# Reordering the first transfers of a hybrid attention/RWKV block: token rows and first weights first, vector rows from ScalarE's queue, unit blocks and bias rows later

## The chip, the cores and the metric

The kernel runs on one core of a Trainium2 chip. The metric is the device time of one execution in microseconds (us). Before the change it is 3353.46 us, the median of three runs (3352.36 to 3354.02). A core has TensorE (matmul, "PE"), VectorE ("DVE"), ScalarE ("ACT"), GpSimd ("POOL") and SyncE ("SP"), which here only issues DMA transfers. ScalarE and GpSimd issue some transfers too. All engines run their own instruction list in order and wait for each other by semaphores.

## The reference

One layer for 2048 tokens of width 1024: a norm, one projection to 5376 columns, chunk-band attention and an RWKV-7 recurrence on its parts, a gated merge, and a feed-forward part.

```python
h = rms_norm(x, pre_mix_g)
proj = h @ w_in                                  # 1024 x 5376
p_att, p_rwkv, p_gate = columns of proj          # 1536, 1792, 2048
y_a = chunk_band_attention(p_att, rel_bias)      # bias by clipped distance
y_b = rwkv7_time_mix(p_rwkv, shift_mu, w0, w2, a0, a2, g2, k_k, k_a, r_k, ln_x_w, ln_x_b)
merged = sigmoid(gate_a) * (y_a @ proj_a) + sigmoid(gate_b) * (y_b @ proj_b)
x = x + rms_norm(merged @ w_out, post_mix_g)
x = x + rms_norm(relu(rms_norm(x, pre_ffn_g) @ w_up)**2 @ w_down, post_ffn_g)
```

## The kernel before

The tokens are worked in four groups of 512 (`G`). For each group the kernel keeps the normed tokens h transposed in SBUF, split into a rounded part and its rest (`hh`, `hl`), and multiplies them with weight blocks of 128 columns. A weight block is 512 KB. SyncE loads it into a buffer `raw` (two of them), ScalarE casts it to `whi` (line 69), VectorE subtracts to `wlo` (line 70), and TensorE adds up 3 x 8 products of 128x128 by 128x512 in one PSUM bank `psd` (line 78): `hh,whi`, `hl,whi` and `hh,wlo` for each of the eight parts of 128 rows. There are two buffers each of `raw`, `whi` and `wlo`, so the load of a block waits until VectorE has read the block two before it, and its cast waits until TensorE is through with that block. Each transfer also uses one of eight completion counters (DMAHW0 to DMAHW7), which are given out in turn over the queues of SyncE and ScalarE; a transfer is not issued before the last one on its counter has landed.

Where a group starts, `phase_norm` loads four tiles of 128 token rows and the gains `g_pre` (each 512 KB), ScalarE sums the squares (line 303), GpSimd makes `rs_r` from them (lines 123 and 125), VectorE scales the tile in place (line 306), TensorE transposes it (line 144), ScalarE casts to `hh` (line 146) and VectorE subtracts to `hl` (line 147). Only the first group does this at the start of the program; for the other groups it lies beside earlier work.

`constants` builds what the mixing needs. It loads nine vectors as rows of one tile `rows` (line 216), which TensorE transposes into `cst` (line 225); the small matrices w2 and a2 (line 223); eight parts of `x0`, a block of unit columns by which the triangular inverse starts (line 242; ScalarE copies it to `X` at line 535); and, in `build_bias`, eight copies of 384 KB that spread each head's bias row 128 times in DRAM (`skew`, line 898), from which the attention phase reads its bias tiles much later.

After that `phase_rwkv` runs for the group. Its first column blocks are the low-rank inputs (`lora_wa`, column block 12, called block 1 below), then r, k and v of head pair 0 (blocks 2 to 4), two gate blocks (5 and 6), and r, k and v of pair 1 (7 to 9); block 10 is the next gate block. From block 1 come `lw` and `lora`, which the small products `ps_z` and `ps_a` (lines 355 and 356) need; from `ps_z` come `tw`, a scan over it (line 396) and `E` (line 400).

A scheduler orders each engine's instructions by its own estimates, within what the data and the buffers allow. So the place of an instruction in its engine's list is not always its place in the code.

Of the kernel before, what the change touches and what calls it, by code (L numbers as in the profile page):

```python
# [8 lines left out]
F32 = mybir.dt.float32  # L9
# [8 lines left out]
P = 128  # L18
D = 1024
# [4 lines left out]
G = 512  # L24
GT = G // P
# [15 lines left out]
RW0 = 1536  # L41
# [3 lines left out]
def advance(steps, n=None):  # L45

    while n is None or n > 0:
        if next(steps, steps) is steps:
            return
        n = n and n - 1  # L50


class Block:
# [5 lines left out]

    def wsplit(self, src, k, n):  # L60

        raw = self.wp.tile([P, k, n], F32, tag="raw", name="wraw")
        self.nc.sync.dma_start(raw, src)
        hi, lo = (self.wp.tile([P, k, n], F32R, tag="w" + x, name="w" + x) for x in ("hi", "lo"))
        self.split(hi, lo, raw)
        return hi, lo
# [41 lines left out]
    def dense(self, col):  # L108


        if self.g == 0:
            self.order.append(col)
            wh, wl = self.wsplit(*self.block(col))
        else:
            wh, wl = next(self.feed)
        ps = self.pd.tile([P, G], F32, tag="d", name="psd")
        self.mm = self.mm3(ps, [(wh[:, k], wl[:, k], self.h[0][:, k], self.h[1][:, k]) for k in range(KB)])
        return ps
# [31 lines left out]
    def constants(self, ctx, mixing):  # L150
        tc, nc, a = self.tc, self.nc, self.a
# [53 lines left out]
        with tc.tile_pool(name="setup", bufs=1, side="right") as sp, \  # L205
# [5 lines left out]
            )  # L211
            yield
            raw = sp.tile([nrow, P], F32, name="rows")
            at, off = 0, {}
            for name, n in rows:
                nc.sync.dma_start(raw[at : at + n], a[name].rearrange("(n p) -> n p", p=P))
                off[name] = at
                at += n
            raw2 = []
            for x in ("w2", "a2"):  # L220
# [7 lines left out]
            for par in range(2):  # L228
# [6 lines left out]
                )  # L235
            self.build_bias(sp, dp)
            eyeb = sp.tile([2, 512], BF16, name="eyeb")
            nc.vector.tensor_copy(eyeb, eye.rearrange("p r j -> p (r j)"))
            eyed = dp.tile([2, 512], BF16, name="eyed")
            nc.sync.dma_start(eyed, eyeb)  # L240
            for i in range(8):
                nc.sync.dma_start(
                    self.x0[i * 16 : i * 16 + 16].rearrange("p r j -> p (r j)"),
                    eyed[i % 2][None, :].to_broadcast((16, 512)),
                )

        def view(name, n):
# [47 lines left out]

    def norm_steps(self, g, sp, pt, gt, t):

        nc = self.nc
        x = sp.tile([P, D], F32, tag="x", bufs=GT, name="x")
        nc.sync.dma_start(x, self.a["x"][g * G + t * P : g * G + (t + 1) * P])  # L300
        sq = sp.tile([P, D], F32, tag="sq", bufs=1, name="sqx")
# [11 lines left out]
    def phase_norm(self, g, sp, pt):  # L313

        gt = self.gain(sp, self.a["pre_mix_g"], "g_pre")
        for t in range(GT):
            advance(self.norm_steps(g, sp, pt, gt, t))

# [53 lines left out]
    def rwkv_pre(self, g, p, rp, NA, between=lambda: None):  # L372
        nc = self.nc
# [17 lines left out]
        self.mix(g, 8 + p, v)  # L391

        between()
        nc.vector.tensor_scalar(tw, tw, -0.5 * DEC, -0.5 * DEC, ALU.mult, ALU.add)
# [490 lines left out]
    def build_bias(self, sp, dp):  # L885
# [10 lines left out]
        nc.sync.dma_start(band, ext)  # L896
        for h in range(8):
            nc.sync.dma_start(
                self.skew[h].rearrange("(q m) -> q m", m=769)[:, 0:768], band[h][None, :].to_broadcast((P, 768))
            )  # L900

# [577 lines left out]
    def run(self):  # L1479
        tc, e = self.tc, None  # L1480
        with ExitStack() as ctx, ExitStack() as mixing:
            e = mixing.enter_context
            consts = self.constants(ctx, mixing)
            advance(consts, 1)
            self.pd = ctx.enter_context(tc.tile_pool(name="pd", bufs=2, space=PSUM))
            self.wp = e(tc.tile_pool(name="w", bufs=2))
# [83 lines left out]
```

## Time and profile before

| | |
|---|---|
| median of three runs | 3353.46 us (3352.36 to 3354.02) |
| the profiled execution's own time | 3355.02 us |
| its span, first to last instruction | 3353.1 us |
| mean granted TensorE clock | 0.991 |
| moved by DMA | 478.42 MB, mean 143 GB/s |
| eight `skew` copies | 384.0 KB each, issued by SyncE |

The page divides the span into 40 slices and gives the busy tenths of each engine in each. A row of a group or of the timeline names line, engine, operation, out<-in and shape; what stands in square brackets is the time that the engine was idle before it, and the instruction or transfer that ended this idle time. In the rows of stretches the columns are: the stretch and its length, busy time and count for PE, PEld, DVE, ACT and POOL, the granted TensorE clock, the busy share of the DMA engines, and GB/s. A row with SPq is the issue of a transfer on SyncE, not the transfer.

### The profile page before, as it was taken

How to read it: one execution, taken by the hardware profiler on the slowest of the kernel's cores; microseconds unless marked ns; L12 is line 12 of the kernel's file. 1: busy time of each engine (PE TensorE's matmuls, PEld its weight loads, DVE VectorE, ACT ScalarE, POOL GpSimd, SP SyncE). 2: the span in 40 equal slices, each digit the busy share in tenths (PEclk: the TensorE clock that was granted, in tenths of full speed). 3: DMA queues.
4: the chain of work that ended last, by engine and by line, in shares of the span. 5: the costliest groups of instructions: out<-in, count | busy, mean ns of one | idle time of the engine just before them, and what ended most of it. 6: DMA issues, size and time to landing. Idle time of an engine off the chain costs nothing. (4 is left out here: it accounts for less than half of the span.)

```text
span 3353.1 us, 49354 instructions
## 1 busy us (share of the span) xinstructions
PE 3254.7 (97%) x19089; PEld 2612.5 (78%) x19089; DVE 2281.7 (68%) x3806; ACT 1461.6 (44%) x2331; POOL 391.8 (12%) x732
## 2 busy tenths in 40 slices
PE   7999999999999999999999999999999999999998
PEld 5777777777777778777777777888887877888886
DVE  5774656675665774665774675876877777776778
ACT  3434634444644434644434644333331254454432
POOL 2110002110012210012210000111200011100002
PEclk9999999999999999999999999999999999999999
DMA  4224343125364224354224266334755364554443
GB/s 150 86 78 149 105 138 117 64 95 175 97 222 133 76 86 165 107 203 151 83 82 152 86 216 228 131 115 141 269 174 200 109 240 162 171 169 154 148 154 126
DMA packets 164945, 478.42 MB, mean 143 GB/s; under 512 B 17436, under 2 KB 34016, under 8 KB 162024
## 3 DMA queue, kind: packets, MB, share of 16 engines
q1 hardware_dynamic: 110120, 364.10, 33.3%
q0 software_dynamic: 18688, 63.98, 4.9%
q10 hardware_dynamic: 35904, 47.20, 3.9%
q8 instruction: 151, 2.47, 0.3%
q14 instruction: 82, 0.67, 0.1%
HBM read 355.64 MB, written 122.71 MB: 143 GB/s over the span
## 5 line engine op out<-in xcount | busy, mean ns | idle before, releaser
L78 PE MATMUL psd<-hh,whi 128*128 128x512 f32 x1344 | 545.2, 406 | 8.9 <-ACT whi L69 6.6
L78 PE MATMUL psd<-hl,whi 128*128 128x512 f32 x1344 | 541.6, 403 | 0.0
L78 PE MATMUL psd<-hh,wlo 128*128 128x512 f32 x1344 | 539.4, 401 | 0.6 <-DVE wlo L70 0.5
L69 ACT CAST whi<-wraw 128x1024 fp32r<-128x1024 f32 x232 | 243.5, 1050 | 530.7 <-PE psd L78 423.2
L78 PE MATMUL ps_dn<-fop 128*128 128x512 f32 x1920 | 440.7, 390 | 3.5 <-DVE u L1267 2.9
L70 DVE TENSOR_TENSOR wlo<-wraw,whi 128x1024 fp32r<-128x1024 f32 x232 | 283.0, 1220 | 213.5 <-ACT whi L69 193.8
L78 PEld LDWEIGHTS ps_dn<-fop 128*128 128x128 f32 x1920 | 359.0, 188 | 81.3 <-DVE u L1267 4.9
L78 PEld LDWEIGHTS psd<-hh,whi 128*128 128x128 f32 x1344 | 257.1, 191 | 65.1 <-ACT whi L69 7.4
L78 PEld LDWEIGHTS psd<-hh,wlo 128*128 128x128 f32 x1344 | 257.0, 191 | 56.6 <-issue 3.5
L78 PEld LDWEIGHTS psd<-hl,whi 128*128 128x128 f32 x1344 | 257.1, 191 | 51.3 <-issue 2.1
L78 PE MATMUL ps_dn<-fop,fop 128*128 128x512 f32 x1008 | 228.6, 389 | 0.0
L78 PEld LDWEIGHTS ps_dn<-fop,fop 128*128 128x128 f32 x1008 | 189.2, 188 | 39.3
L1267 DVE TENSOR_TENSOR u<-u,ps_dn 128x512 f32<-128x512 f32 x240 | 160.0, 682 | 51.9 <-PE ps_dn L78 51.2
L868 DVE CUSTOM_DVE_ANT_0 sc<-bias,ps_s 128x640 f32<-128x640 f32 (+4 forms) x128 | 94.1, 735 | 55.4 <-PE ps_s L862 47.1
L69 ACT CAST fop<-wdraw 128x1024 fp32r<-128x1024 f32 x40 | 41.9, 1047 | 191.4 <-DVE u L1267 106.9
L873 ACT ACTIVATE sc<-sc,mn 128x640 f32<-128x640 f32 (+4 forms) x128 | 97.8, 764 | 35.3 <-DVE mn L868 30.1
L69 ACT CAST s12h<-s 128x1024 fp32r<-128x1024 f32 x32 | 33.7, 1053 | 169.4 <-PE ps_u L78 164.6
L995 PE MATMUL ps_o<-whi,mh 128*128 128x512 f32 x256 | 102.6, 401 | 2.4 <-ACT o L1001 2.4
L995 PE MATMUL ps_o<-wlo,mh 128*128 128x512 f32 x256 | 102.3, 400 | 0.5 <-DVE wlo L70 0.4
L78 PE MATMUL ps_p<-yh,whi 128*128 128x512 f32 x256 | 101.9, 398 | 0.6 <-DVE th L961 0.6
L78 PE MATMUL ps_p<-yh,wlo 128*128 128x512 f32 x256 | 102.2, 399 | 0.0
L995 PE MATMUL ps_o<-whi,ml 128*128 128x512 f32 x256 | 101.7, 397 | 0.0
(378 smaller groups left out, 6751.1 us busy)
## 6 DMA issues: line engine op xcount, KB each, us to landing
wraw<-in_w_in_dram SPq DMA_DIRECT2D x168, 512.0 KB
wraw<-in_w_up_dram SPq DMA_DIRECT2D x80, 512.0 KB
ar<-sd SPq DMA_DIRECT2D x21, 1024.0 KB
wdraw<-in_w_down_dram SPq DMA_DIRECT2D x40, 512.0 KB
araw<-ad SPq DMA_DIRECT2D x40, 512.0 KB
gd<-gate ACTq DMA_DIRECT2D x64, 256.0 KB
wraw<-in_w_out_dram SPq DMA_DIRECT2D x32, 512.0 KB
ad<-r POOLq DMA_DIRECT2D x64, 256.0 KB, 2.7
```

Source lines behind the costliest of these rows:

```text
L69: self.nc.scalar.copy(hi, src)
L70: self.nc.vector.tensor_tensor(lo, src, hi.bitcast(F32), ALU.subtract)
L78: mm = nc.tensor.matmul(ps, l, r, start=start and n == 0, stop=stop and n == last).ins
L868: nc.vector.tensor_tensor_reduce(sc[:, 0:n], bias[:, s0:640], pss[:, c0 : c0 + n], 1.0, 3.0e38, ALU.add, ALU.min, mn,)
L873: nc.scalar.activation(sc[:, 0:n], sc[:, 0:n], AF.Exp, scale=-1.0, bias=mn, accum_out=sm)
L995: nc.tensor.matmul(ps[t], l[:, k, ts], r[:, k % 2], start=k == 0 and j == 0, stop=k == KB - 1 and j == 2)
L1267: nc.vector.tensor_tensor(u[t][:, ns], u[t][:, ns], ps, ALU.add)
```

## The change

The load of a weight block and its split are parted, so that the load can be written earlier than the split. `phase_norm` now issues the four token tiles, then the gains, then the loads of blocks 1 and 2, and splits these blocks after the norm. The nine vector rows are issued by ScalarE instead of SyncE, ahead of all other work of ScalarE. The eight `x0` copies and the eight `skew` copies go into a generator `spread` that `rwkv_pre` runs for head pairs 0 and 1 of the first group: `x0` for pair 0 and `skew` for pair 1, each batch placed behind the weight load that was written last. The products, their count and the order of the weight blocks stay.

```diff
...
         self.NG = self.S // G
 
 
-    def wsplit(self, src, k, n):
-
+    def wload(self, src, k, n):
         raw = self.wp.tile([P, k, n], F32, tag="raw", name="wraw")
-        self.nc.sync.dma_start(raw, src)
+        self.loaded = self.nc.sync.dma_start(raw, src).ins
+        return raw, k, n
+
+    def wsplit(self, *block):
+        return self.wparts(*self.wload(*block))
+
+    def wparts(self, raw, k, n):
         hi, lo = (self.wp.tile([P, k, n], F32R, tag="w" + x, name="w" + x) for x in ("hi", "lo"))
         self.split(hi, lo, raw)
         return hi, lo
...
 
         if self.g == 0:
             self.order.append(col)
-            wh, wl = self.wsplit(*self.block(col))
+            wh, wl = self.first.pop(col, None) or self.wsplit(*self.block(col))
         else:
             wh, wl = next(self.feed)
         ps = self.pd.tile([P, G], F32, tag="d", name="psd")
...
             nc.gpsimd.affine_select(
                 eye, eye, [[1, 32], [-2, 16]], ALU.is_equal, 0.0, base=0, channel_multiplier=-1
             )
-            yield
             raw = sp.tile([nrow, P], F32, name="rows")
             at, off = 0, {}
             for name, n in rows:
-                nc.sync.dma_start(raw[at : at + n], a[name].rearrange("(n p) -> n p", p=P))
+                nc.scalar.dma_start(raw[at : at + n], a[name].rearrange("(n p) -> n p", p=P))
                 off[name] = at
                 at += n
+            yield
             raw2 = []
             for x in ("w2", "a2"):
                 raw2.append(sp.tile([P, HW], F32, name="raw2"+x))
...
                 nc.vector.tensor_tensor(
                     self.wl[par][r], raw2[par][r], self.wh[par][r].bitcast(F32), ALU.subtract
                 )
-            self.build_bias(sp, dp)
+            band = self.build_bias(sp, dp)
             eyeb = sp.tile([2, 512], BF16, name="eyeb")
             nc.vector.tensor_copy(eyeb, eye.rearrange("p r j -> p (r j)"))
             eyed = dp.tile([2, 512], BF16, name="eyed")
             nc.sync.dma_start(eyed, eyeb)
+
+        def spread():
             for i in range(8):
                 nc.sync.dma_start(
                     self.x0[i * 16 : i * 16 + 16].rearrange("p r j -> p (r j)"),
                     eyed[i % 2][None, :].to_broadcast((16, 512)),
                 )
+                yield
+            for h in range(8):
+                nc.sync.dma_start(
+                    self.skew[h].rearrange("(q m) -> q m", m=769)[:, 0:768], band[h][None, :].to_broadcast((P, 768))
+                )
+                yield
+
+        self.spread = spread()
 
         def view(name, n):
             return self.cst[:, off[name] : off[name] + n]
...
         lo = self.hp.tile([P, KB, G], F32R, tag="hl", name="hl")
         return hi, lo
 
-    def norm_steps(self, g, sp, pt, gt, t):
+    def norm_load(self, g, sp, t):
+        x = sp.tile([P, D], F32, tag="x", bufs=GT, name="x")
+        self.nc.sync.dma_start(x, self.a["x"][g * G + t * P : g * G + (t + 1) * P])
+        return x
+
+    def norm_steps(self, g, sp, pt, gt, t, x=None):
 
         nc = self.nc
-        x = sp.tile([P, D], F32, tag="x", bufs=GT, name="x")
-        nc.sync.dma_start(x, self.a["x"][g * G + t * P : g * G + (t + 1) * P])
+        if x is None:
+            x = self.norm_load(g, sp, t)
         sq = sp.tile([P, D], F32, tag="sq", bufs=1, name="sqx")
         ssq = sp.tile([P, 1], F32, tag="ssq", bufs=4, name="ssq")
         nc.scalar.activation(sq, x, AF.Square, accum_out=ssq)
...
 
     def phase_norm(self, g, sp, pt):
 
+        xs = [self.norm_load(g, sp, t) for t in range(GT)]
         gt = self.gain(sp, self.a["pre_mix_g"], "g_pre")
+        first = [(col, self.wload(*self.block(col))) for col in (RW0 + 12 * P, RW0)]
         for t in range(GT):
-            advance(self.norm_steps(g, sp, pt, gt, t))
+            advance(self.norm_steps(g, sp, pt, gt, t, xs[t]))
+        for col, w in first:
+            self.first[col] = self.wparts(*w)
 
 
     def mix(self, g, blk, out):
...
         v = self.tmp("v")
         self.mix(g, 8 + p, v)
 
+        if g == 0 and p < 2:
+            with self.tc.issue_after(self.loaded):
+                advance(self.spread, 8)
         between()
         nc.vector.tensor_scalar(tw, tw, -0.5 * DEC, -0.5 * DEC, ALU.mult, ALU.add)
         cum = tw
...
         nc.vector.tensor_scalar(ext[:, 383:703], ext[:, 383:703], -1.0, None, ALU.mult)
         nc.vector.tensor_copy(ext[:, 0:383], ext[:, 383:384].to_broadcast((8, 383)))
         nc.sync.dma_start(band, ext)
-        for h in range(8):
-            nc.sync.dma_start(
-                self.skew[h].rearrange("(q m) -> q m", m=769)[:, 0:768], band[h][None, :].to_broadcast((P, 768))
-            )
+        return band
 
     def load_bias(self, h):
         nc = self.nc
...
             e = mixing.enter_context
             consts = self.constants(ctx, mixing)
             advance(consts, 1)
+            self.first = {}
             self.pd = ctx.enter_context(tc.tile_pool(name="pd", bufs=2, space=PSUM))
             self.wp = e(tc.tile_pool(name="w", bufs=2))
             self.hp = e(tc.tile_pool(name="h", bufs=1))
```

The order of the instructions moves at three places. The first is the head of SyncE's list, before the change:

```order
L134 DMA g_pre_134<-in_pre_mix_g_dram 128x1024
L300 DMA x_136<-in_x_dram 128x1024
L300 DMA x_162<-in_x_dram 128x1024
L300 DMA x_186<-in_x_dram 128x1024
L300 DMA x_210<-in_x_dram 128x1024
L216 DMA rows_236<-in_gate_bias_dram 16x128
L216 DMA rows_236<-in_shift_mu_dram 14x128
L216 DMA rows_236<-in_w0_dram 4x128
L216 DMA rows_236<-in_a0_dram 4x128 [waits DMAHW0_49]
L216 DMA rows_236<-in_k_k_dram 4x128 [waits DMAHW1_49]
L216 DMA rows_236<-in_k_a_dram 4x128 [waits DMAHW2_49]
L216 DMA rows_236<-in_r_k_dram 4x128 [waits DMAHW3_49]
```

and with it (`wraw_154` and `wraw_156` are blocks 1 and 2, `wraw_497` and `wraw_540` blocks 3 and 4):

```order
L313 DMA x_144<-in_x_dram 128x1024
L313 DMA x_146<-in_x_dram 128x1024
L313 DMA x_148<-in_x_dram 128x1024 [waits DMAHW1_49]
L313 DMA x_150<-in_x_dram 128x1024 [waits DMAHW4_49]
L139 DMA g_pre_152<-in_pre_mix_g_dram 128x1024 [waits DMAHW5_49]
L62 DMA wraw_154<-in_w_in_dram 128x1024 [waits DMAHW6_49]
L62 DMA wraw_156<-in_w_in_dram 128x1024 [waits DMAHW7_49]
L228 DMA raw2w2_258<-in_w2_dram 64x512 [waits DMAHW0_49]
```

Since ScalarE's nine rows now take counters between SyncE's transfers, the third token tile has the counter of the first (DMAHW1), the fourth that of the row a0 (DMAHW4), and the gains that of the second tile (DMAHW5). The two weight loads stood at rows 21 and 22 of the list before and stand at rows 6 and 7 now.

The second place is further down on SyncE, where the `skew` copies stood ahead of the load of block 3 (`wraw_513` before):

```order
L898 DMA skew_261<-band_262 128x768 [waits DMAHW6_49,DMAHW1_49]
L898 DMA skew_261<-band_262 128x768 [waits DMAHW7_49]
L898 DMA skew_261<-band_262 128x768 [waits DMAHW0_49]
L898 DMA skew_261<-band_262 128x768
L898 DMA skew_261<-band_262 128x768 [waits DMAHW2_49]
L898 DMA skew_261<-band_262 128x768 [waits DMAHW3_49]
L898 DMA skew_261<-band_262 128x768 [waits DMAHW4_49]
L898 DMA skew_261<-band_262 128x768 [waits DMAHW5_49]
L242 DMA x0_104<-eyed_279 16x512 [waits DMAHW6_49]
L63 DMA wraw_513<-in_w_in_dram 128x1024 [waits DMAHW7_49,DVE_49]
```

Now they stand behind the load of block 9 (`wraw_845`) and ahead of that of block 10 (`wraw_1016`):

```order
L62 DMA wraw_802<-in_w_in_dram 128x1024 [waits DMAHW4_49,DMAHW2_49,DVE_49]
L62 DMA wraw_845<-in_w_in_dram 128x1024 [waits DMAHW6_49,DMAHW3_49,DVE_49]
L255 DMA skew_273<-band_274 128x768 [waits DMAHW7_49]
L255 DMA skew_273<-band_274 128x768 [waits DMAHW0_49]
L255 DMA skew_273<-band_274 128x768 x2
L255 DMA skew_273<-band_274 128x768 [waits DMAHW4_49]
L255 DMA skew_273<-band_274 128x768 [waits DMAHW5_49]
L255 DMA skew_273<-band_274 128x768 [waits DMAHW6_49]
L255 DMA skew_273<-band_274 128x768 [waits DMAHW7_49]
L62 DMA wraw_1016<-in_w_in_dram 128x1024 [waits DMAHW0_49,DVE_49]
```

The load of block 10 has the counter of the second copy (DMAHW0).

The third place is ScalarE's list from the first weight casts to the first `E`. Before (`whi_426` and `whi_472` are blocks 1 and 2, `whi_515` and `whi_558` blocks 3 and 4):

```order
L69 CAST whi_426<-wraw_424 128x1024
L69 CAST whi_472<-wraw_470 128x1024
L325 COPY pr_455<-psd_430 128x512
L328 ACTIVATE lw_423<-psd_430,omu_291 128x512
L342 ACTIVATE lw_423<-lw_423 64x512
...
L328 ACTIVATE r_469<-psd_476,omu_291 128x512
L383 ACTIVATE tw_510<-ps_z_507,hw0_295 128x512
L400 ACTIVATE E_595<-tw_510 128x8x64
L535 CAST X_997<-x0_104 128x512
L69 CAST whi_515<-wraw_513 128x1024
L69 CAST whi_558<-wraw_556 128x1024
```

and now (`whi_248` and `whi_252` are blocks 1 and 2, `whi_499` and `whi_542` blocks 3 and 4):

```order
L74 CAST whi_248<-wraw_154 128x1024
L151 CAST hh_166<-pstr_168 128x4x128
L151 CAST hh_166<-pstr_175 128x4x128
L74 CAST whi_252<-wraw_156 128x1024
...
L74 CAST whi_499<-wraw_497 128x1024
L349 COPY pr_445<-psd_420 128x512
L352 ACTIVATE lw_419<-psd_420,omu_287 128x512
L562 CAST X_997<-x0_104 128x512
L366 ACTIVATE lw_419<-lw_419 64x512
L372 CAST lora_455<-lw_419 64x512
L372 CAST lora_452<-lw_419 64x512
L74 CAST whi_542<-wraw_540 128x1024
```

The casts of blocks 1 and 2 moved from behind all `hh` casts to between them, and on VectorE their subtractions stand ahead of the last `hl` pairs in the same way; the cast of block 3 moved from behind `E` and `X` to ahead of the copy of block 1's sum, and `X` moved into the chain of `lw`. On TensorE, `ps_z` now stands two products into block 3 and `ps_a` later, where both stood ahead of block 3 before.

## The prediction

> **What bounds the kernel now.** I read the page first, then who waited for whom in the first 200 us, then the timeline around the longest wait.
>
> ```profile
> span 3353.1 us, 49354 instructions
> PE 3254.7 (97%) x19089; PEld 2612.5 (78%) x19089; DVE 2281.7 (68%) x3806; ACT 1461.6 (44%) x2331; POOL 391.8 (12%) x732
> PE   7999999999999999999999999999999999999998
> ```
>
> TensorE is busy for 97% and only its first slice of 84 us falls to 0.7, so a change that touches the first 70 us can win what TensorE loses there, and not more. Behind the first blocks the instruction order of all engines is the same in both kernels, so what is won early arrives at the end as a shift.
>
> TensorE's waits in the first 200 us (total, times, longest):
>
> ```profile
> PE pstr L144 <- DVE x L306: 10.1, 1, 10.1
> PE psd L78 <- ACT whi L69: 6.6, 2, 4.9
> PE pstr L144 <- DVE hl L147: 3.6, 3, 2.6
> PE ps_t L569 <- DVE X L548: 2.8, 1, 2.8
> ...
> PE psd L78 <- DVE wlo L70: 0.5, 1, 0.5
> ```
>
> The 6.6 us are two waits for a weight cast: 1.62 before block 1 (the first 128-column weight block) and 4.95 before block 3. The timeline (start, duration, engine, line) has both:
>
> ```profile
> 23.44 0.79 PE L78 MATMUL psd<-hh,whi 128*128 128x512 f32 x1 [1.62 <-ACT whi L69]
> ...
> 33.07 0.36 SPq L63 DMA_DIRECT2D wraw<-in_w_in_dram  x1
> ...
> 41.82 0.63 ACT L400 ACTIVATE E<-tw 128x512 f32<-128x512 f32 x1 [1.90 <-DVE tw L396]
> 42.36 0.60 ACT L535 CAST X<-x 128x512 f32<-128x512 bf16 x1
> 42.87 2.23 ACT L69 CAST whi<-wraw 128x1024 fp32r<-128x1024 f32 x2
> 43.96 0.79 PE L78 MATMUL psd<-hh,whi 128*128 128x512 f32 x1 [4.95 <-ACT whi L69]
> ```
>
> The cast of block 3 is held twice over. On ScalarE it stands behind E and X, which wait for VectorE's scan. And its load was issued only at 33.07, behind the eight bias-row copies, and landed hardly before 42.87, as the stretches show (engines' busy times, granted clock, DMA share, GB/s):
>
> ```profile
> 23.44:29.63 6.19, 5.65 (x12) 4.00 (x13) 2.79 (x7) 0.89 (x1) 0.00 (x0) 1.00 0.48 121
> 29.63:38.99 9.36, 9.36 (x41) 7.38 (x39) 2.12 (x3) 3.87 (x7) 0.47 (x3) 1.00 1.03 235
> 43.96:50.08 6.12, 6.08 (x14) 4.30 (x15) 2.40 (x2) 1.05 (x1) 0.00 (x0) 0.50 0.55 171
> ...
> 26.00:43.00 17.00, 13.01 (x49) 10.18 (x48) 5.23 (x8) 5.98 (x11) 1.29 (x5) 1.00 0.96 246
> 43.00:44.00 1.00, 0.04 (x1) 0.04 (x1) 0.24 (x2) 0.91 (x1) 0.23 (x1) 0.70 0.10 41
> ```
>
> The DMA engines are 96% busy from 26 to 43 and fall to 0.10 in the next microsecond. Removing one of the two holds alone would win next to nothing; the change removes both. The pause has a second price: the granted clock falls inside 43 to 44 and stays at 0.50, so 14 matmuls take 6.12 us, where 41 take 9.36 before it (0.228 each).
>
> **The change, part by part.** First, block 3's wait. Its load now stands directly behind the first two blocks' loads and needs only the buffer of block 1, which VectorE frees near 19 us. A transfer into an idle queue takes 4.2 us (next fence), so it lands near 24 and is needed after 35. Its cast now stands ahead of the copy of block 1's sum; E and X no longer hold it. This gives back 4.95 us. Not free: the cast (1.05 us) now delays the low-rank chain that TensorE meets two matmuls into block 3.
>
> ```profile
> 32.67 0.59 ACT L325 COPY pr<-psd 128x512 f32<-128x512 f32 x1 [8.34 <-PE psd L78]
> ...
> 34.67 0.63 ACT L342 ACTIVATE lw<-lw 64x512 f32<-64x512 f32 x1 [0.82 <-DVE lw L329]
> 35.97 1.41 DVE L349 TENSOR_TENSOR lora<-lw,lora 64x512 fp32r<-64x512 f32 x2 [1.34 <-ACT lora L348]
> ```
>
> The chain took 32.67 to 37.38, 4.7 us; with the cast 5.75. Block 2 and two matmuls cover 26 x 0.228 = 5.9. X (0.60) moves into the 0.82 that ScalarE spends waiting for VectorE. I take 0, and 0.6 as the cost if X does not fit.
>
> Second, the slow stretch. Without the pause the 14 matmuls take 14 x 0.228 = 3.2 instead of 6.12: 2.9 us.
>
> Third, the start.
>
> ```profile
> 0.80 0.40 SPq L134 DMA_DIRECT2D g_pre<-in_pre_mix_g_dram  x1
> 1.25 1.94 SPq L300 DMA_DIRECT2D x<-in_x_dram  x4
> 3.23 0.74 SPq L216 DMA_DIRECT2D rows<-in_gate_bias_dram  x1
> ...
> 5.09 0.25 SPq L216 DMA_DIRECT2D rows<-in_a_dram  x1
> 6.38 0.25 SPq L216 DMA_DIRECT2D rows<-in_k_k_dram  x1
> 7.67 0.25 SPq L216 DMA_DIRECT2D rows<-in_k_a_dram  x1
> 8.95 0.25 SPq L216 DMA_DIRECT2D rows<-in_r_k_dram  x1
> ...
> 8.72 1.28 DVE L306 SCALAR_TENSOR_TENSOR x<-x,rs_r,g_pre 128x1024 f32<-128x1024 f32 x1 [3.33 <-POOL rs_r L125]
> ...
> 22.47 0.69 DVE L147 TENSOR_TENSOR hl<-pstr,hh 128x512 fp32r<-128x512 f32 x1 [0.16 <-ACT hh L146]
> ```
>
> The rows a0, k_k, k_a and r_k wait for the counters of g_pre and token tiles 1 to 3, so they show when those land: 5.0, 6.3, 7.6, 8.9. That is 4.2 us for the first transfer and 1.28 for each that follows without a break. Now the tiles come first, but the third waits for the counter of the first, and the gains come fifth. Lower bound, no break: the fifth lands where it did, at 10.2. Upper bound, the third is issued at 5.0 and again takes 4.2: 9.2, 10.5, 11.8. I take 11.0, the middle. So VectorE begins to scale later than now (8.72), and from there it is the bound: by group it has
>
> ```profile
> L147 DVE TENSOR_TENSOR hl<-pstr,hh 128x512 fp32r<-128x512 f32 x8 | 5.4, 687 | 0.4 <-ACT hh L146 0.3
> L306 DVE SCALAR_TENSOR_TENSOR x<-x,rs_r,g_pre 128x1024 f32<-128x1024 f32 x4 | 5.1, 1282 | 4.8 <-POOL rs_r L125 4.0 <-DMA rows<-in_k_a_dram 0.7
> L70 DVE TENSOR_TENSOR wlo<-wraw,whi 128x1024 fp32r<-128x1024 f32 x2 | 2.4, 1222 | 0.0
> ```
>
> 4 x 1.28 + 8 x 0.69 + 2 x 1.22 = 13.1, now without the 4 us of waits for rs_r, which is ready long before the gains. The last hl ends near 24.1. The first matmul that needs an hl of the last tile can go one hl earlier, at 23.4, with two hh products of 0.44 ahead of it: TensorE starts at 22.5, and both weight parts are there. Before, it started at 23.44 and lost another 0.54 to wlo. Gain 1.5, by the bounds 0.7 to 2.3. The vector rows on ScalarE win nothing of their own: nine issues of 0.25 to 0.74 (3.0 together) and the table load of 1.28 end near 5.1, as the first tile lands; they would cost only once the squares slip past 11. The two weight casts among the hh casts lie inside ScalarE's waits for transposes.
>
> Fourth, the bias rows, moved behind the ninth weight load.
>
> ```profile
> 25.59 5.25 SPq L898 DMA_DIRECT2D skew<-band  x8
> ...
> 68.83 0.33 SPq L63 DMA_DIRECT2D wraw<-in_w_in_dram  x1
> ...
> 89.20 1.05 ACT L69 CAST whi<-wraw 128x1024 fp32r<-128x1024 f32 x1 [0.70 <-PE psd L78]
> 95.13 1.05 ACT L69 CAST whi<-wraw 128x1024 fp32r<-128x1024 f32 x1 [3.23 <-PE psd L78]
> ```
>
> The ninth load goes out at 68.83, after a shift of 9.35 at 59.5. From the first copy to the landing of the two loads behind it took 25.59 to 43.0, 17.4 us; the tenth load then lands at 77. The 256-KB stores of ScalarE and GpSimd fall into this stretch: three of them at 246 GB/s add 3.1, so 80. Block 10's matmuls begin when block 9's end, 95.13 less 9.35 = 85.8, and its cast takes 1.05. The copies are hidden with 4 to 5 us to spare; each us of landing after 84.7 costs one. The unit-block rows (16 KB each) land near 30, before X is cast near 33.
>
> Sum: 1.5 + 4.95 + 2.9 = 9.35. The profiled execution took 3355.02, so 3345.7. It was 1.56 slower than the median of the timed runs, 3353.46, so part of the slow stretch may be missing in those; I put the forecast at 3345.6.
>
> **The rivals.** B: the slow stretch is chance. The clock fell only within 43 to 44, after more than 4 us of the 4.95; in another execution the pause may end before it falls. For it:
>
> ```profile
> 140.00:160.00 20.00, 17.20 (x187) 13.61 (x186) 17.75 (x38) 13.71 (x22) 3.38 (x8) 0.91 0.19 53
> ```
>
> here the clock fell with a longest wait of 2.8 us (ps_t), so length alone does not decide. If the timed runs before mostly kept their clock, the gain is 1.5 + 4.95 = 6.45: 3347.0 from the median, no change by the bound below. [...]
>
> C: the start gets later. If every transfer behind the second pays a break of its own (4.2 instead of 1.28 once more), the gains land near 14.5, the start loses 2 us instead of winning 1.5, and the time is 3349. For it: tile 3 waits for tile 1 and the gains for tile 2; against it: tile 4 waits only for a small row.
>
> D, the other side: the copies starve the weight loads. Place: the tenth load, SyncE's queue behind them. If the copies run at half the rate beside the stores, their 3.1 MB take 25 us instead of 12.8 and the load lands at 93: TensorE waits 8 us, the clock falls again (2.9), and the time is 3357. It decides from a landing at 84.7; to be slower by 0.2% the load must land near 97. Against it: the measured 246 GB/s are of these same copies, beside two loads.
>
> **How the numbers follow.** Forecast 0.57, B 0.25, C 0.12, D 0.06. About 0.2%, 6.7 us, is what a measurement tells from no change: faster is below 3346.8. The forecast's own range is 3343.5 to 3347.5; with B and C, 3342 to 3351 leaves out most of D and the ends. Nearly all of the forecast and a third of B and C are faster: 0.63; D is slower in two thirds: 0.05; the rest, 0.32, is the same.
>
> **What would show it.** The first scale of VectorE at 10 to 12 us and the first psd matmul at 21.7 to 23.3; no TensorE wait for whi over 1 us; full clock from about 29 us on; the skew copies issued near 60 and the tenth cast released by TensorE, not by its load. A first matmul after 24, a wait in block 3 or block 10, or a copy still running past 85 would make it wrong.

## The result and the profile after

The changed kernel takes 3343.30 us (median of 8 runs, 3341.57 to 3346.92), the kernel before beside it 3353.53 us (8 runs, 3351.46 to 3355.03). The ratio is 0.9974, with a 95% interval of 0.9966 to 0.9983: faster by 10.2 us between the medians. The profiled execution took 3342.12 us, with a span of 3340.3 us.

The waits of TensorE in the first 200 us of the changed kernel (total, times, longest):

```profile
PE ps_rows L230 <- POOL rs_v L128: 9.3, 1, 9.3
PE pstr L149 <- DVE x L326: 5.8, 1, 5.8
PE ps_t L596 <- DVE X L575: 2.8, 1, 2.8
PE pstr L149 <- DVE hl L152: 2.5, 3, 1.4
```

No row for `whi` is left: the 6.6 us of before are gone. The rows above lie ahead of the first product, except `ps_t`. The timeline of the changed kernel, from the start to block 10:

```profile
5.05 1.61 SPq L313 DMA_DIRECT2D x<-in_x_dram  x2
6.16 0.25 ACTq L220 DMA_DIRECT2D rows<-in_ln_x_b_dram  x1
6.44 1.28 ACT L323 ACT_TABLE_LOAD   x1 [6.44 <-DMA rows<-in_w_dram]
6.71 0.43 SPq L139 DMA_DIRECT2D g_pre<-in_pre_mix_g_dram  x1
14.11 3.68 DVE L326 SCALAR_TENSOR_TENSOR x<-x,rs_r,g_pre 128x1024 f32<-128x1024 f32 x3 [3.06 <-DMA g_pre<-in_pre_mix_g_dram]
25.67 1.22 PE L83 MATMUL psd<-hh,whi 128*128 128x512 f32 x2
33.52 1.05 ACT L74 CAST whi<-wraw 128x1024 fp32r<-128x1024 f32 x1 [7.05 <-PE psd L83]
44.93 1.05 ACT L74 CAST whi<-wraw 128x1024 fp32r<-128x1024 f32 x1 [1.00 <-PE psd L83]
61.96 7.13 SPq L255 DMA_DIRECT2D skew<-band  x8
69.98 20.54 SPq L62 DMA_DIRECT2D wraw<-in_w_in_dram  x4
81.92 1.05 ACT L74 CAST whi<-wraw 128x1024 fp32r<-128x1024 f32 x1 [0.70 <-PE psd L83]
```

And its stretches (busy times of PE, PEld, DVE, ACT and POOL, granted clock, DMA share, GB/s):

```profile
29.80:38.69 8.89, 8.89 (x40) 7.34 (x39) 2.71 (x4) 4.50 (x8) 0.94 (x2) 1.00 0.23 69
46.00:52.00 6.00, 6.00 (x28) 4.96 (x27) 3.44 (x5) 2.77 (x5) 1.50 (x3) 1.00 0.33 89
82.00:84.00 2.00, 2.00 (x10) 1.64 (x9) 1.00 (x1) 2.00 (x4) 0.06 (x2) 1.00 0.01 2
```

Three things are to be seen. Block 3's cast (33.52) is released by TensorE, the clock stays full behind it, and 28 matmuls go through in 46 to 52 us. The copies are hidden: the tenth cast is released by TensorE at 81.92, and from 82 to 84 us the DMA engines stand at 0.01. But the start got later, not earlier: the first scale comes at 14.11 in place of 8.72, the first `psd` product at 25.67 in place of 23.44.

A clean mark for what the first blocks won is the tenth cast, which in both kernels waits for nothing but TensorE: 89.20 before, 81.92 after, so 7.28 us. The profiled executions are 12.9 us apart. The other 5.6 us are won later, in places that the change does not touch; the second profiles below show that differences of this size come between executions of one kernel.

### The profile page after: what moved, and what is told of

Its sections match the earlier page's. It is cut to its first block, busy times and chain, and to the rows that moved or that the text cites. A ratio compares the mean times of both kernels' runs of the same rounds, so it can differ in the third digit from the quotient of the medians.

```text
span 3340.3 us, 49351 instructions
## 1 busy us (share of the span) xinstructions
PE 3247.1 (97%) x19089; PEld 2609.9 (78%) x19089; DVE 2282.6 (68%) x3806; ACT 1462.3 (44%) x2331; POOL 391.8 (12%) x732
```

## Experiments

All times are medians, and each ratio is to the kernel before on the same chip in the same session. "Shift" is 89.20 minus the tenth cast in the profile, "full clock" where the granted clock first stays at 1.00 behind the start.

| version | us (runs) | ratio, 95% interval | first psd | full clock | tenth cast | shift |
|---|---|---|---|---|---|---|
| before, first profile | 3353.53 (8) | 1 | 23.44 | 29.75 | 89.20 | 0 |
| before, second profile | 3354.31 (1) | | 22.91 | 28.99 | 88.58 | 0.62 |
| the change | 3343.30 (8) | 0.9974, 0.9966 to 0.9983 | 25.67 | 30.06 | 81.92 | 7.28 |
| the change, again | 3346.31 (11) | 0.9976, 0.9968 to 0.9985 | 25.89 | 28.47 | 81.28 | 7.92 |
| late copies alone | 3343.43 (5) | 0.9964, 0.9952 to 0.9977 | 22.78 | 29.08 | 80.73 | 8.47 |
| the change without late copies | 3348.89 (11) | 0.9977, 0.9968 to 0.9986 | 26.12 | 27.34 | 81.83 | 7.37 |
| vector rows on SyncE | 3341.51 (5) | 0.9961, 0.9948 to 0.9973 | 21.66 | 26.32 | 78.75 | 10.45 |
| vector rows on SyncE, again | 3342.51 (6) | 0.9968, 0.9956 to 0.9980 | 22.13 | 20.55 | 77.06 | 12.14 |
| gains first | 3344.18 (6) | 0.9968, 0.9956 to 0.9980 | 23.77 | 25.24 | 78.72 | 10.48 |
| rows on SyncE and gains first | 3343.86 (6) | 0.9968, 0.9956 to 0.9980 | 22.37 | 27.97 | 79.86 | 9.34 |
| cast of block 3 held | 3351.15 (10) | 0.9994, 0.9985 to 1.0003 | 26.34 | 29.57 | 89.33 | -0.13 |
| load of block 3 held | 3357.71 (10) | 1.0011, 1.0002 to 1.0020 | 25.06 | 22.44 | 93.05 | -3.85 |
| copies twice | 3355.70 (1) | | 25.11 | 22.55 | 91.36 | -2.16 |

**Late copies alone.** The kernel before, with nothing but the unit blocks and bias rows moved into `spread`:

```diff
-            self.build_bias(sp, dp)
+            band = self.build_bias(sp, dp)
...
+        if g == 0 and p < 2:
+            with self.tc.issue_after(self.loaded):
+                advance(self.spread, 8)
```

> The kernel before, with only the late unit blocks and bias rows of the change. Theory (the gain is the late copies alone: 4.95 of wait and 2.9 of slow clock; the new head of the program, with first transfers and vector rows moved, loses about 0.6): the first psd product starts at 23.4 as before, block 3 has no wait over 1 us, the cast of block 5 runs at 44 to 45 (52.67 before, 44.93 with the whole change), and the time is that of the whole change or 1 us less: 3341 to 3345. Rival (the forecast's: first transfers win 1.5 of the gain): the cast of block 5 runs at 46 to 47 and the time is 1.5 to 2 us above the whole change, 3345 to 3347.

Rows of its timeline:

```profile
22.78 0.80 PE L78 MATMUL psd<-hh,whi 128*128 128x512 f32 x1 [1.62 <-ACT whi L69]
24.74 1.46 SPq L63 DMA_DIRECT2D wraw<-in_w_in_dram  x2
60.73 7.64 SPq L250 DMA_DIRECT2D skew<-band  x8
80.73 1.05 ACT L69 CAST whi<-wraw 128x1024 fp32r<-128x1024 f32 x1 [0.70 <-PE psd L78]
```

This part alone gives 8.47 us, more than the whole change. The start is that of before (the 1.62 for `whi` too), and the wait at block 3 and the slow stretch behind it are gone. Of the 8.47, some 0.6 are scatter of the start: the first product comes at 22.78, as in the second profile of before (22.91), and against that profile's tenth cast the shift is 88.58 - 80.73 = 7.85, which is the 4.95 and 2.9 of the prediction. The two profiles of the change have their tenth cast 1.19 and 0.55 us later than this version. So the new order of the start won nothing where the prediction had it win 1.5.

**The change without late copies.** The copies are issued in `constants` again; all else as changed.

```diff
         self.spread = spread()
+        advance(self.spread)
...
-        if g == 0 and p < 2:
-            with self.tc.issue_after(self.loaded):
-                advance(self.spread, 8)
```

> The whole change without its last part: unit blocks and bias rows are issued where the constants are built. Since the loads of blocks 1 and 2 come first, the loads of blocks 3 and 4 still stand ahead of the copies in SyncE's list. Theory (what counts is that the load and the cast of block 3 are not behind the copies and E): no wait in block 3, the load of block 5 lands near 43 to 46 and is needed near 45 to 50, time within 2 us of the whole change, 3341 to 3346. Rival (copies of 3.1 MB early in the program cost their 8 us wherever TensorE meets them): TensorE waits 4 us or more at block 5, the clock falls, and the time is 3349 to 3354.

```profile
48.68 1.05 ACT L74 CAST whi<-wraw 128x1024 fp32r<-128x1024 f32 x1 [2.50 <-DMA wraw<-in_w_in_dram]
81.83 1.05 ACT L74 CAST whi<-wraw 128x1024 fp32r<-128x1024 f32 x1 [0.70 <-PE psd L83]
```

The loads of blocks 3 and 4 now go out at 23.74, ahead of the copies, and block 3 does not wait. The load of block 5 is late behind the copies (its cast at 48.68 waits for it), but of that TensorE sees 0.3 us. The shift is 7.37, that of the change. The median, 3348.89, lies outside the 3341 to 3346 that were expected, but the kernel before was slower beside these runs too (3355.68), and the ratio of 0.9977 is that of the change (0.9974 and 0.9976). What matters is that block 3's load stands ahead of the copies; that the copies go 30 us later is not needed for it.

**Vector rows on SyncE.** The nine rows go back to SyncE, behind the two weight loads; token rows and copies as changed.

```diff
+            yield
             raw = sp.tile([nrow, P], F32, name="rows")
...
-                nc.scalar.dma_start(raw[at : at + n], a[name].rearrange("(n p) -> n p", p=P))
+                nc.sync.dma_start(raw[at : at + n], a[name].rearrange("(n p) -> n p", p=P))
...
-            yield
```

> The whole change, but the nine vector rows are again issued by SyncE, behind the two weight loads. No transfer among the first seven then waits for a counter. Theory (the counters that the ScalarE rows take make tiles 3 and 4 and the gains wait, which delays the first scale to 14.1): the gains land at 10.2 to 11.8, the first psd product starts at 21.7 to 23.3 (25.67 with the whole change) and the time is 2 to 4 us below the whole change, 3339 to 3342. Rival (the gains are late because they are fifth and slow, whoever issues the rows): first scale at 13 to 14, first psd product at 25 to 26, time that of the whole change, 3342 to 3345.

Its timeline (two rows of transfers, the first scale, first product, tenth cast):

```profile
0.80 1.82 SPq L313 DMA_DIRECT2D x<-in_x_dram  x4
2.66 0.49 SPq L139 DMA_DIRECT2D g_pre<-in_pre_mix_g_dram  x1
10.22 3.68 DVE L326 SCALAR_TENSOR_TENSOR x<-x,rs_r,g_pre 128x1024 f32<-128x1024 f32 x3 [4.84 <-DMA g_pre<-in_pre_mix_g_dram]
21.66 1.22 PE L83 MATMUL psd<-hh,whi 128*128 128x512 f32 x2 [0.83 <-ACT hh L151]
78.75 1.05 ACT L74 CAST whi<-wraw 128x1024 fp32r<-128x1024 f32 x1 [0.70 <-PE psd L83]
```

All four token tiles and the gains are issued by 3.15, without a wait, where the change issues the third tile at 5.05 and the gains at 6.71. The gains land at 10.2 in place of 14.0. In the change the DMA engines are half idle from 9 to 11 us; this stretch, first of the change, then of this version:

```profile
9.00:11.00 2.00, 0.33 (x1) 0.18 (x1) 1.33 (x12) 1.97 (x3) 1.71 (x5) 1.00 0.48 184
```
```profile
9.00:11.00 2.00, 0.00 (x0) 0.00 (x0) 0.78 (x1) 0.99 (x2) 1.42 (x4) 1.00 1.02 393
```

So it was the rows of ScalarE that made the start late: nine small transfers of 2 to 8 KB use up the eight counters, so that in the trace of the change the third tile waits 3.4 us for the counter of the first and the fourth 0.9 us for that of a row. Why the DMA engines are half idle from 9 to 11 us, when the gains and both weight loads have been issued by 8.1, is not shown.

A second set of runs of the same version was to show whether the time follows:

> Once more the change with the vector rows on SyncE behind the two weight loads, to see whether the 3.2 us that its trace won over the change up to the tenth cast (78.75 against 81.92) are there in the time of more executions. Theory (the start repeats, the half-clock stretches further on are chance): first psd product at 21.7 to 22.5, tenth cast at 78.7 to 79.9 depending on when the clock rises, median 3341 to 3344, ratio to the kernel before 0.9962 to 0.9970. Rival (what the start wins is taken back further on, as in the version with the gains ahead of the tiles, 3343.9): median 3344 to 3346.

It did: 3342.51, and the tenth cast even at 77.06. Products of block 1 that follow each other, first of the first profile, then of the second:

```profile
23.96 0.63 PE L83 MATMUL psd<-hh,wlo 128*128 128x512 f32 x1
24.39 0.63 PE L83 MATMUL psd<-hh,whi 128*128 128x512 f32 x1
```
```profile
23.60 0.39 PE L83 MATMUL psd<-hh,whi 128*128 128x512 f32 x1
23.83 0.40 PE L83 MATMUL psd<-hl,whi 128*128 128x512 f32 x1
```

A product begins every 0.43 us in the one and every 0.23 in the other: where the clock was at full speed from 20.55 on, the tenth cast comes 1.7 us earlier with the same order, although the first product is 0.5 later. (In the first profile the clock's records begin only at 26.32; the spacing of the products shows what was granted ahead of that.) By its two ratios, 0.9961 and 0.9968, this is the best version tried, but its intervals overlap those of the change.

**Gains first.** The change with `g_pre` ahead of the token tiles, once with the rows on ScalarE, once with the rows on SyncE:

```diff
-        xs = [self.norm_load(g, sp, t) for t in range(GT)]
         gt = self.gain(sp, self.a["pre_mix_g"], "g_pre")
+        xs = [self.norm_load(g, sp, t) for t in range(GT)]
```

> The whole change, but the gains are issued ahead of the four token tiles. Theory (the first scale is late because the gains come last of the five): the first scale starts at 10 to 11, bound by the squares that now start at 7.7 behind ScalarE's rows and table load, the first psd product at 21.5 to 23, time 3339 to 3342. Rival (the counters set it): the fourth tile now lands at about 14, its scale stands at 15 to 16, the products start at 24 to 26 and the time is 3342 to 3345.

> The change with the vector rows on SyncE behind the two weight loads and with the gains ahead of the token tiles. Theory (the completion counters that the nine row issues of ScalarE take make the third tile and the gains late, and in the version with rows on SyncE the gains, landing at 10.2, are all that is left): with the gains first the first scale starts near 8.7 as in the kernel before, VectorE works from there without a break, the first psd product comes at 20.5 to 21.0, and the tenth cast at 77.9 to 78.2, 11 to 11.5 us earlier than before. Rival (the last token tile and its transposes, not the gains, set the start once the counters are free): the first scale moves to 8.7 but the first product stays at 21.7 and the tenth cast at 78.7, as with rows on SyncE alone. Time by the first 3341, by the second 3341.5; both lie inside the 3 to 5 us by which the half-clock stretches further on differ between executions, so the trace decides and not the time.

Rows of the first of them, then of the second:

```profile
9.86 1.26 DVE L326 SCALAR_TENSOR_TENSOR x<-x,rs_r,g_pre 128x1024 f32<-128x1024 f32 x1
23.77 1.22 PE L83 MATMUL psd<-hh,whi 128*128 128x512 f32 x2
```

```profile
9.02 1.28 DVE L326 SCALAR_TENSOR_TENSOR x<-x,rs_r,g_pre 128x1024 f32<-128x1024 f32 x1 [3.63 <-POOL rs_r L130]
22.37 1.22 PE L83 MATMUL psd<-hh,whi 128*128 128x512 f32 x2 [0.68 <-ACT hh L151]
79.86 1.05 ACT L74 CAST whi<-wraw 128x1024 fp32r<-128x1024 f32 x1 [0.69 <-PE psd L83]
```

With the gains first and the rows on ScalarE the first scale comes at 9.86, but the first product only at 23.77, with the last tile's scale at 16.66; that lies between the theory (21.5 to 23) and the rival (24 to 26), and the time of 3344.18 is the rival's. Its tenth cast, 78.72, is as early as with the rows on SyncE, but here the full clock came 1.5 us behind the first product, in the change 4.4; how much of the 3.2 us is the order and how much the clock stays open. With the rows on SyncE as well, the first scale comes at 9.02 and the first product still at 22.37: there the rival was right. With the counters free the last tile and its transposes set the start here (TensorE's last wait ahead of the first product is 0.68 us for `hh`), and moving the gains wins nothing (22.37 against 21.66).

**Block 3's two holds, one at a time.** First the cast: the load stays early, but the scan and E of pair 0 are written ahead of block 3, and its cast behind E, so that on ScalarE E and then two casts follow each other as before (X now stands further ahead, at 37.70). `hold` is the instruction that makes E.

```diff
+            with self.tc.issue_after(self.hold):
+                self.nc.scalar.copy(hi, src)
```

> The change with one of block 3's two holds put back: the load stays where the change has it (landed near 18 to 24), but on ScalarE the cast of block 3 is written behind X and E again, and E behind VectorE's scan. Theory (each hold alone is enough to keep TensorE waiting): block 2 ends near 37.7 to 38.7, E follows some 3.7 us later and the cast behind it, so TensorE waits 4.5 to 5.5 us for whi at 39 to 44, the tenth cast comes at 86 to 90 in place of 81.9, and the time is 5 to 8 us above the change: 3348 to 3351. Rival (it was the load alone; the scheduler put the cast behind E because the load was late): the cast waits behind E but TensorE loses under 1.5 us, and the time stays at 3343 to 3345.

Timeline, and the stretches on both sides of the clock's fall:

```profile
42.81 0.63 ACT L420 ACTIVATE E<-tw 128x512 f32<-128x512 f32 x1 [1.91 <-DVE tw L416]
43.35 1.03 ACT L76 CAST whi<-wraw 128x1024 fp32r<-128x1024 f32 x1
44.43 0.80 PE L88 MATMUL psd<-hh,whi 128*128 128x512 f32 x1 [4.46 <-ACT whi L76]
89.33 1.05 ACT L79 CAST whi<-wraw 128x1024 fp32r<-128x1024 f32 x1 [0.69 <-PE psd L88]
```
```profile
39.81:43.22 3.41, 0.16 (x1) 0.00 (x0) 2.31 (x3) 1.50 (x3) 0.43 (x2) 1.00 0.00 0
43.22:46.63 3.41, 2.16 (x4) 1.33 (x5) 2.91 (x3) 2.10 (x3) 0.72 (x1) 0.50 0.02 5
```

The load landed at 27.5, some 16 us ahead of its cast, and still TensorE waits 4.46 us and the gain is gone (ratio 0.9994). The tenth cast is 89.33 - 81.92 = 7.41 us later than in the change: 4.46 for the wait, and the other 2.95 are nearly all the half clock behind it (0.17 of them are a later block 1). That is a direct price for the two largest terms of the prediction together.

Then the load: the copies early, block 3's load behind all of them, its cast ahead of E. `copied` is the last bias-row copy, `third` the cast of block 3.

```diff
+                with self.tc.issue_after(self.copied):
+                    w = self.wload(*self.block(col))
...
+            with self.tc.issue_after(self.third):
+                nc.scalar.activation(E[:, :, 1 : C + 1], cum3, AF.Exp)
```

> The change with the other of block 3's two holds put back: the unit-block and bias-row copies are issued in constants and the load of block 3 behind all of them, while on ScalarE the cast of block 3 stands ahead of E. Theory (either hold alone keeps TensorE waiting, since in the kernel before the load landed at 42.8, as late as E let the cast go): the load lands near 43 to 45, TensorE waits 4 to 6 us for whi in block 3 with the cast released by its load, the granted clock falls to half behind this wait as in the three executions so far that had one of 4.5 to 5.1 us, and the tenth cast comes at 88 to 90. With block 3's cast held behind E alone it was 89.3 and the median 3351.2, so 3349 to 3353 here. Rival (most of the wait was the place of the cast, and the load alone costs little): TensorE waits under 2 us, tenth cast at 82 to 84, 3343 to 3347.

```profile
30.31 5.06 SPq L261 DMA_DIRECT2D skew<-band  x8
47.65 1.04 ACT L74 CAST whi<-wraw 128x1024 fp32r<-128x1024 f32 x1 [9.02 <-DMA wraw<-in_w_in_dram]
48.75 0.80 PE L83 MATMUL psd<-hh,whi 128*128 128x512 f32 x1 [11.05 <-ACT whi L74]
```

The kind is as expected, the size is not: the copies start at 30.31 here (25.59 in the kernel before), so the load lands at 47.65, TensorE waits 11.05 us, and the time is 3357.71 in place of 3349 to 3353. Either hold alone is enough for the wait, and the load's is not the smaller one. In the kernel before they ended together: by the trace the load's counter takes its last step at 42.81, and the cast behind E and X begins at 42.87.

**Copies twice.** Behind the ninth load the eight bias rows are spread twice, first into a second buffer that nothing reads.

```diff
-            for h in range(8):
+            for h in range(16):
                 nc.sync.dma_start(
-                    self.skew[h].rearrange("(q m) -> q m", m=769)[:, 0:768], band[h][None, :].to_broadcast((P, 768))
+                    (self.skew2, self.skew)[h // 8][h % 8].rearrange("(q m) -> q m", m=769)[:, 0:768], band[h % 8][None, :].to_broadcast((P, 768))
```

> The change with the eight bias-row copies written twice behind the ninth weight load (the first eight go into a second buffer in DRAM that nothing reads), 6.2 MB in place of 3.1. This measures the cover that the prediction put at 4 to 5 us. In the change the copies are issued from 62.0, the tenth load is issued at 70.0, and block 10's matmuls begin at 87.9. Theory (copies and the loads behind them share some 250 GB/s): the tenth load lands 12.6 us later, near 91 to 93, block 10's cast is released by its load, TensorE waits 4 to 7 us there, the clock may fall behind it, and the time is 4 to 9 us above the change, 3348 to 3354. Rival (loads and copies run side by side in different DMA rings, so a load is not delayed by the copies ahead of it): the tenth load lands within 5 us of its issue, no wait of TensorE for whi over 1 us, and the time is that of the change.

```profile
59.92 20.38 SPq L255 DMA_DIRECT2D skew<-band  x16
91.36 1.04 ACT L74 CAST whi<-wraw 128x1024 fp32r<-128x1024 f32 x1 [9.46 <-DMA wraw<-in_w_in_dram]
92.46 0.80 PE L83 MATMUL psd<-hh,whi 128*128 128x512 f32 x1 [6.47 <-ACT whi L74]
```

The tenth load lands at 91.36, where it landed at 80.7 in the change, and TensorE waits 6.47 us: behind sixteen copies the load was late enough for what rival D describes, and the change avoids it only by its margin. Here block 10 would have started at 92.46 - 6.47 = 85.99. With half the copies (3.1 MB less, 12.8 us at the 246 GB/s of the prediction's row) the load would land near 78.6, where 84.9 was needed: a cover of about 6 us, an estimate from these rows. The trace of the change agrees: the 80.7 is the last step of the tenth load's counter there, and block 10's products begin at 87.9, so the cast had to begin by 86.8. The wait and the half clock behind it together exceed what was expected of the time (3355.70 against 3348 to 3354; a single run).

**Both kernels again.** What of the surplus behind block 10 belongs to the kernel?

> The kernel before once more. The first 43 us repeat (first psd product near 23.4, cast of block 3 near 42.9, TensorE wait 4.95). [...]

> The change itself once more, beside the others on one chip. Theory (the half-clock stretches behind block 10 fall where the clock's periods of 3.4 us happen to lie against the kernel's pauses, so they belong to the execution and not to the kernel): the first 100 us repeat to 0.3 us (first psd product 25.7, tenth cast 81.9, no TensorE wait for a cast in block 3), while the list of half-clock stretches behind block 10 is another one than in the first profile (9 stretches, 40.9 us in all, the first at 245 us), with a total anywhere between 30 and 48 us, and the median of the runs is 3341 to 3347. Rival (the change moved these stretches for good): the same places again within a few us, a total of 40 to 42, and 3343.3 within 1.

The kernel before, second profile (first product of block 3, and the stretch behind it):

```profile
43.59 0.79 PE L78 MATMUL psd<-hh,whi 128*128 128x512 f32 x1 [5.13 <-ACT whi L69]
46.00:52.00 6.00, 6.00 (x21) 4.79 (x20) 0.02 (x1) 0.00 (x0) 0.00 (x0) 0.71 0.51 167
```

Wait and slow stretch are there again. The change's second profile repeats the first 90 us (81.28 against 81.92), but its execution took 3349.94 us, 7.8 more than the first. The same 10 us of both, far behind the change's edits, the first profile first:

```profile
2733.00:2743.00 10.00, 10.00 (x46) 8.29 (x45) 9.31 (x11) 7.08 (x11) 0.00 (x0) 1.00 0.85 338
```
```profile
2733.00:2743.00 10.00, 8.39 (x30) 6.75 (x31) 7.30 (x8) 8.15 (x12) 0.00 (x0) 0.83 0.99 372
```

The first granted the full clock here, the second half a clock from 2735.2 to 2738.6, and 46 matmuls against 30 got through. From 2530 to 2860 us TensorE waits 7.1 us for ScalarE and VectorE in the second, 3.5 in the first. The half-clock stretches behind block 10 are not a new list, as had been expected: of the nine in the first profile of the change eight come back within 6 us in the second, and of the ten of the kernel before eight within 1 us. What differs is which of the others come and whether one lasts 3.41 or 6.83 us (in the change 40.9 us in all against 44.4), and the waits beside them. Such differences fall out anew in each execution: the 19 runs of the change spread from 3341.2 to 3350.8, and the 23 of the kernel before in one session from 3347.1 to 3360.6. So 6.7 to 7.9 us belong to the change by the two profiles of each kernel (88.58 - 81.92 to 89.20 - 81.28), and what the first comparison shows above that (12.9 in the profiles, 10.2 in the medians) is of the size of this scatter; the second comparison, 7.4 us between medians of 11 and 23 runs, has hardly any of it.

## Why the prediction was right or wrong

The time of 3345.6 lies between the two medians of the change, 3343.30 and 3346.31. Both are inside the wide range of 3342 to 3351; the first is 0.2 below the forecast's own range of 3343.5 to 3347.5. But one term of the sum, the start, won nothing, and scatter in the first comparison made up for it: that the time fits so well is partly luck.

- **Block 3's wait, 4.95: right.** It is gone, and with one hold put back 4.46 of it returns. That either hold alone would keep it is shown by the two runs, in the kind for both and in the size for the cast. The lora chain cost nothing: X moved into ScalarE's gap (35.53 to 36.15) and TensorE has no wait for `ps_z`. The load went out at 23.29 and not near 19, which cost nothing, since it was needed only at 33.52.
- **The slow stretch, 2.9: right, and rival B falls.** Five executions had a wait of TensorE for a cast of 4.46 to 11.05 us (both profiles of before, the two holds, the copies twice), and in all five the clock fell to half behind it, for 6.8 or 10.2 us. With the cast held, the stretch is worth 2.95. B had the stretch missing in most executions. The half-clock records of the 13 traces last 3.41 us or multiples of it, but for the last of each trace, which ends with it. In the first profiles of both kernels they also begin a whole number of 3.41 us apart (before at 43.40, 152.63 and 255.03, which is 32 and 30 times 3.413), so the traces can be cut into periods of this length. In both profiles of before the wait held a wholly idle period, so these two alone leave open what a wait does that holds none; but the traces show that less is enough. These are stretches of one period each, of the kernel before (first two) and of the change:

```profile
39.99:43.40 3.41, 0.00 (x0) 0.00 (x0) 2.46 (x4) 1.58 (x3) 0.97 (x2) 1.00 0.90 312
149.19:152.60 3.41, 1.48 (x66) 1.40 (x67) 3.38 (x7) 1.36 (x3) 0.18 (x1) 1.00 0.59 159
```
```profile
142.70:146.11 3.41, 2.26 (x69) 2.04 (x70) 3.38 (x6) 2.13 (x4) 0.18 (x1) 1.00 0.56 159
```

  Behind the first and the second the clock fell, though in the second TensorE was busy for 1.48 of 3.41 us; behind the third, with 2.26, it did not. The 13 traces, cut into their periods of 3.41 us and counted, give: of the periods at full clock, all 105 with TensorE busy for less than 0.40 had half the clock behind them, of the 152 from 0.40 to 0.70 there were 30, and of the more than 12000 above 0.70 none. A wait of 4.95 us puts at least half of itself into one period, so that period is busy for at most 0.27 of its length, wherever the periods lie. By this count the stretch was not chance.
- **The start, +1.5: wrong, it won nothing.** In the first profiles it cost 0.85 (ScalarE goes on from block 1 at 33.52 against 32.67). That size is not firm, since it hangs on the clock too: in the six profiles with this start the last product of block 1 ends at 31.34 to 33.61 us, 32.50 on the mean, in the three with the old start at 32.04 to 32.63, 32.25 on the mean. What repeats is the later first product, 25.06 to 26.34 against 22.78 to 23.44. Rival C had the place, and a loss of 2.

  The step that failed is "The vector rows on ScalarE win nothing of their own", where their issues were counted as time of ScalarE and not as users of the counters, together with the upper bound of 11.8 for the gains, which let only the third tile wait. In the trace tile 3 waits for tile 1 (issued 5.05), tile 4 for a row (6.34, its counter's row landed at 6.32), the gains behind them go out at 6.71 and land at 14.0, 7.3 us later and past both bounds. ScalarE's own last rows wait as well, so that its table load comes at 6.44 and not at 3.8. With the rows on SyncE the gains land at 10.2 and the first product comes at 21.66, at the near end of what the forecast had named (21.7 to 23.3). The first product is 2.23 us later, yet the loss is smaller, since 0.5 of wait for `wlo` falls away and the half clock at the start is shorter (25.67 to 30.06 in place of 23.44 to 29.75).
- **The copies hidden, with 4 to 5 us to spare: right.** The skew copies go out from 61.96, the tenth cast is released by TensorE, and the doubled copies put the cover at about 6.
- **The sum.** 4.95 + 2.9 - 0.85 (block 1 ends at 33.52 against 32.67) = 7.0 stands against a shift of 7.28, where 9.35 was forecast. That the first comparison shows 10.2 to 12.9 owes to differences behind block 10, and the second profile of the change shows that these come between executions of one kernel. Two slips of the prediction's working change nothing: three stores of 256 KB at 246 GB/s take 3.2 us, not 3.1, and two thirds of D's 0.06 are 0.04, not 0.05.

## What to carry to other kernels

A transfer put on another engine's queue was not free here, where the two queues share completion counters: count how many are issued before the first large ones have landed, since nine rows of 2 to 8 KB held back 512-KB loads (the third tile by 3.4 us) and the tenth cast came some 3 us later than with the same rows behind those loads (81.92 against 78.75). Where an engine waits, list everything that would hold the waiting instruction, by order and by data; here two holds ended within 0.1 us of each other (42.81 and 42.87), and putting either back took all of the gain (ratios 0.9994 and 1.0011). And compare early marks of the trace, not only times: a shift of 7.3 us was read to 0.6 us in the first 90 us of two profiles, while the whole time moves by 7.8 between them.

## What the runs showed that was not expected

- The granted clock fell behind every period of 3.41 us in which TensorE was busy for less than 0.40 of it (105 of 105). By this count a single wait of more than 4.1 us (twice 0.6 of a period) would lower it wherever the periods lie, an estimate; behind the wait of 4.46 us this cost 2.95 us more. Behind a wait of 2.8 us (`ps_t` near 143 to 153 us) the clock fell in the first profile of before, at 152.63, and not in that of the change.
- The clock first stays at 1.00 behind the start from between 20.55 and 30.06 us on in 13 traces, and from between 22.44 and 30.06 in the six that have the start of the change. Between two profiles of one kernel (26.32 and 20.55) the tenth cast differs by 1.7 us (78.75 and 77.06). In the first profiles of both kernels the full clock begins a whole number of periods ahead of the first fall behind it (29.75 and 43.40, 4 periods; 30.06 and 245.10, 63 periods); that its place hangs on where the periods happen to lie is the author's guess, not shown apart.
- A 512-KB transfer issued behind others that waited took 7.3 us to land (the gains of the change, 6.71 to 14.0), and 4.2 into an idle queue (those of before, 0.80 to 5.0); in the change the DMA engines stood at 0.48 from 9 to 11 us.
